# First MLP product ahead of the last two norms, a convolution's layer norm in two halves, and ties of a search counted from squared signs

## The chip, the cores and the metric

The kernel runs on one core of a Trainium2 chip. The metric is the device time of one execution in microseconds (us). The core has five engines that run side by side, each with its own instruction stream, held together by semaphores: PE (matrix products and transposes; PEld is its weight load), DVE, ACT and POOL (elementwise work), and SP (here only the issue of DMA transfers, in the order of its stream). Matrix products leave their results in eight PSUM banks; everything else lies in SBUF.

## The reference

One layer of a hybrid decoder on 1024 tokens of width 1024, all in float32. `h = rms_norm(x) @ w_in` is cut into inputs of three mixers, whose outputs, side by side, are multiplied by `w_out` and added to `x`; then cross-attention to 256 memory rows; then `x + relu(rms_norm(x) @ w1)**2 @ w2` with a hidden width of 4096.

```
y_a = gated_delta_rule(...)      # 4 heads of 128, chunks of 64, a state carried from chunk to chunk
y_b = sparse attention           # for every query the 256 keys with the largest index score:
      _, sel = lax.top_k(score, 256)              # of equal scores the lower positions win
y_c = silu(layer_norm(causal_depthwise_conv(u * sigmoid(gate), 31 taps) + bias) * g + b)   # 256 channels
x = x + concat(y_a, y_b, y_c) @ w_out
x = x + cross_attention(rms_norm(x), rms_norm(mem))
x = x + square(relu(rms_norm(x) @ w1)) @ w2
```

## The kernel before

**Arithmetic.** Matrix products are done at float32 precision from halves: each operand is split into a high part (a cast on ACT) and a low part (a subtraction on DVE), and `mm3` issues three matmuls for a pair: high by high (L133), first operand's high part by the second's low part (L134), and the first's low part by the second's high part (L135).

**Order.** Tokens are eight tiles `t` of 128 rows. The program is written as Python generators. `weave` interleaves several of them with a rate for each: the one with the higher rate emits more of its steps in the same stretch, and what is emitted first has the higher priority. A scheduler then sets the order on each engine from these priorities and from its own estimate of times; what runs on the chip is that fixed order per engine, and SP's DMA issues have one, too.

**The stretch from 383 to 547 us** is one such weave of four threads: the delta rule's preparation (`gdn_pre`, `gdn_blocks`, `gdn_post`; stages gp and gi, PSUM tag "mg"), the memory rows' norm and projection (`mem_norm`, `mem_stage`; tiles mem_mm, whi, mkv), the last steps of the search for the 256 keys (`topk`), and the convolution with its layer norm (`conv_norm`; the convolution is done with matmuls against diagonal matrices, tile diag). After it, from 547 to 765 us, the sparse attention (stage da) and the delta rule's scan (stage gs) are woven with the projection by `w_out`.

**The end of the search.** For every query block `b` of six, `lo` gets the sign of score minus threshold on ACT (L632), with the row's sum of signs; POOL writes `negm` = 1 where the sign is 0, a tie (L633); DVE makes running counts of ties `cs` (L635), works out how many ties still fit (L637, L638), marks what is left out (L640), and POOL turns it into the mask that is added later (L641). The tile `cs` has one buffer, so that the count of the next block waits for the L641 of the block before.

**The convolution's layer norm** (`conv_norm`): PE transposes the eight token tiles into four PSUM banks (L823), DVE takes mean and variance of each (L825, L826), then one `rsqrt` of ten small DVE instructions (L156 to L168) for all eight, eight scalings (L834), then for each half of four tiles the gain (L835), POOL's bias (L836), ACT's tanh (L838), the gate (L839) and a store `yc_d` (L840). The delta rule's block inverse is beside it on DVE: the chain of tiles `Tb`, `Pb`, `Wb` (L1001 to L1018), whose result is stored as `Xb_d` (L1020). `Ab_d` (L959) is the store, and `Ab` (L988) the load, which feed that chain. Behind the `Xb_d` store SP issues the loads of the attention (KA, VS) and of the scan (lvb, lkd, lqE, lqkT, lkT).

**The MLP** is done in four groups of 1024 hidden units, each as a seven-product scheme on 2 by 2 blocks (`PRODS`, order 1, 2, 5, 6, 3, 7, 4): a product is 48 matmuls of 128x512. `block_sums` makes sums of blocks of the weights (`wsum`) and of the normalised rows (`hsum`); `half` and `rows` split a block for a product (`wm` for weights, `bm` for rows; ACT casts at L1475, DVE subtracts at L1476). In the first group the weights' block sums run on POOL, and the rows' sums on DVE. Token tiles 6 and 7 ("rows 6 and 7") are the last to leave the cross-attention; their norm (n3) ends with transposes (L1412) and copies into the row blocks `h3` (L1415 on DVE, L1417 on ACT). Products 1 and 2 need only token tiles 0 to 3; product 5, the third, and the later ones need tiles 4 to 7 too. `mlp` is a generator that stops after its first product (`next(mlp)`), and rows 6 and 7 are normalised after that stop.

## Time and profile before

| | us |
|---|---|
| three runs | 1609.34, 1612.25, 1613.8 (median 1612.25) |
| the profiled execution | 1610.89 |
| its span, first to last instruction | 1609.2 |
| PE busy | 1513.7 (94%) |
| DVE busy | 1136.0 (71%) |
| ACT busy | 736.2 (46%) |
| POOL busy | 326.7 (20%) |
| mean granted clock of PE | 0.973 |

A row of the timeline gives start, duration, engine, line and operation, the tile written and read, shape, how many instructions are joined in the row, and in square brackets how long the engine was idle before it and what ended that wait. A row of the windows view gives for one stretch the busy time and number of instructions of each engine, PE's granted clock (1.00 is full speed), and the share and rate of DMA. A matmul's own duration overlaps with the next one's, so the pace of PE is read from the starts of its rows or from their number in a stretch in which it never stops.

### The profile page before, as it was taken

Reading aid. Unit: us, or ns where it says so; the run is one execution under the profiler, and the core shown is the slowest. Engines: PE = TensorE matmul, PEld = TensorE weight load, DVE = VectorE, ACT = ScalarE, POOL = GpSimd, SP = SyncE. Lnnn points to the kernel's source line nnn. Section 1 sums busy time; section 2 is a strip of 40 time slices with the busy share of each in tenths; the row PEclk is TensorE's granted clock in tenths of the full one; section 3 lists DMA queues with packets and bytes.
Section 4 is the critical chain, followed back from the end, with each engine's and each line's share of the span. In section 5 each row is a group of like instructions: output and inputs, shape, how many; then the busy total and the mean of one; then the engine's idle time right before and its main releaser. Section 6 shows DMA issues by size and latency. Waiting matters only on the chain.

```text
span 1609.2 us, 20703 instructions
## 1 busy us (share of the span) xinstructions
PE 1513.7 (94%) x7561; PEld 1261.1 (78%) x7561; DVE 1136.0 (71%) x2042; ACT 736.2 (46%) x1375; POOL 326.7 (20%) x279
## 2 busy tenths in 40 slices
PE   6999999998899599999879997999999999999998
PEld 6977888786689488988668876888888888888887
DVE  7649677875665766775667879996469647865783
ACT  4535788676443356664335533332233233323331
POOL 3021444346954222112301104100000000000000
PEclk9999999999899699999999998999999999999999
DMA  6130122121475864435612358713641464147202
GB/s 212 41 98 19 55 79 79 53 80 62 157 233 169 280 209 147 133 102 190 209 54 83 127 188 317 305 47 130 233 167 53 157 226 157 36 157 261 79 13 93
DMA packets 125141, 220.83 MB, mean 137 GB/s; under 512 B 16245, under 2 KB 65134, under 8 KB 117870
## 3 DMA queue, kind: packets, MB, share of 16 engines
q1 hardware_dynamic: 123502, 214.25, 38.9%
q0 software_dynamic: 1536, 5.24, 0.9%
q8 instruction: 60, 0.98, 0.2%
q14 instruction: 43, 0.35, 0.1%
HBM read 158.65 MB, written 60.82 MB: 136 GB/s over the span
## 4 chain that ended last, share of the span: by engine, by line
PE 65%; DVE 14%; ACT 9%; issue 5%; DMA 4%; POOL 3%; SPq 0%; ACTq 0%; POOLq 0%; DVEq 0%
PE mlp_mm L134 13%; PE mlp_mm L135 13%; PE mlp_mm L133 13%; ACT junka L592 4%; DVE acc L748 1%; PE xq_mm L133 1%; PE wa_mm L135 1%; PE wa_mm L133 1%; PE wa_mm L134 1%; PE xw_mm L135 1%; PE xw_mm L133 1%; PE xw_mm L134 1%; PE xq_mm L134 1%; PE xq_mm L135 1%; DVE junk L594 1%
## 5 line engine op out<-in xcount | busy, mean ns | idle before, releaser
L134 PE MATMUL mlp_mm<-bm,wm 128*128 128x512 f32 x448 | 178.5, 399 | 8.0 <-DVE bm L1476 8.0
L133 PE MATMUL mlp_mm<-bm,wm 128*128 128x512 f32 x448 | 177.7, 399 | 2.2 <-ACT bm L1475 1.2
L135 PE MATMUL mlp_mm<-bm,wm 128*128 128x512 f32 x448 | 178.2, 398 | 0.0
L135 PE MATMUL mlp_mm<-wm,am 128*128 128x512 f32 x448 | 177.0, 395 | 0.0
L134 PE MATMUL mlp_mm<-wm,am 128*128 128x512 f32 x448 | 177.0, 395 | 0.0
L133 PE MATMUL mlp_mm<-wm,am 128*128 128x512 f32 x448 | 175.0, 395 | 0.0
L1475 ACT CAST wm<-wq 128x2048 fp32r<-128x2048 f32 x32 | 61.2, 1912 | 211.9 <-PE mlp_mm L134 211.8
L1565 DVE TENSOR_TENSOR xacc<-xacc,mlp_mm 128x512 f32<-128x512 f32 x112 | 75.8, 682 | 69.7 <-PE mlp_mm L135 69.7
L134 PEld LDWEIGHTS mlp_mm<-bm,wm 128*128 128x128 f32 x448 | 85.0, 190 | 29.1 <-DVE bm L1476 8.7
L133 PEld LDWEIGHTS mlp_mm<-bm,wm 128*128 128x128 f32 x448 | 84.9, 190 | 23.3 <-DVE rs_x L156 1.5
L135 PEld LDWEIGHTS mlp_mm<-bm,wm 128*128 128x128 f32 x448 | 85.0, 190 | 20.3
L135 PEld LDWEIGHTS mlp_mm<-wm,am 128*128 128x128 f32 x448 | 84.1, 188 | 20.5
L134 PEld LDWEIGHTS mlp_mm<-wm,am 128*128 128x128 f32 x448 | 84.1, 188 | 20.4
L133 PEld LDWEIGHTS mlp_mm<-wm,am 128*128 128x128 f32 x448 | 84.1, 188 | 20.4
L1476 DVE TENSOR_TENSOR wm<-wsum,wm 128x2048 fp32r<-128x2048 f32 x24 | 59.3, 2472 | 51.3 <-ACT wm L1475 51.3
L1475 ACT CAST wm<-wsum 128x2048 fp32r<-128x2048 f32 x24 | 45.9, 1913 | 106.0 <-PE mlp_mm L134 77.7
L1476 DVE TENSOR_TENSOR wm<-wq,wm 128x2048 fp32r<-128x2048 f32 x32 | 73.3, 2290 | 28.6 <-ACT wm L1475 28.5
L133 PE MATMUL qkv_mm<-hT,whi 128*128 128x512 f32 x192 | 77.7, 404 | 0.9 <-ACT xb L740 0.9
L134 PE MATMUL qkv_mm<-hT,whi 128*128 128x512 f32 x192 | 76.7, 399 | 0.0
L135 PE MATMUL qkv_mm<-hT,wlo 128*128 128x512 f32 x192 | 76.7, 399 | 0.0
L1529 ACT ACTIVATE aq<-mlp_mm 128x512 f32<-128x512 f32 x64 | 37.9, 595 | 68.5 <-PE mlp_mm L135 68.5
L185 POOL TENSOR_TENSOR wlo<-wraw,whi 128x1024 fp32r<-128x1024 f32 x24 | 57.9, 2412 | 3.4 <-issue 1.9
(504 smaller groups left out, 3987.4 us busy)
## 6 DMA issues: line engine op xcount, KB each, us to landing
bm<-hb_d SPq DMA_DIRECT2D x42, 1024.0 KB, 6.5
wq<-in_mlp_w SPq DMA_DIRECT2D x32, 1024.0 KB, 5.3
hb_d<-bm SPq DMA_DIRECT2D x14, 1024.0 KB, 3.9
wraw<-in_w_in SPq DMA_DIRECT2D x20, 512.0 KB, 3.8
qkv_d<-acc SPq DMA_DIRECT2D x12, 512.0 KB, 3.2
...
xa<-in_x SPq DMA_DIRECT2D x16, 256.0 KB, 2.7
```

The source lines that it names most:

```text
L133: mm(out, l[0], r[0], start=start, stop=False, skip_group_check=on)
L134: mm(out, l[0], r[1], start=False, stop=False, skip_group_check=on)
L135: mm(out, l[1], r[0], start=False, stop=stop, skip_group_check=on)
L185: (lo_eng or nc.gpsimd).tensor_sub(lo[:, :n], raw[:, :n], hi[:, :n].bitcast(F32))
L592: Sc.activation(junka[:, :K], X[b], AF.Sign, bias=c, scale=-1.0, accum_out=n)
L594: V.tensor_scalar(junk[:, :K].bitcast(X[b].dtype), X[b], c, None, op0=OP.is_lt, op1=OP.add, accum_out=n)
L748: nc.vector.scalar_tensor_tensor(acc, xb[:, 3 - d:3 - d + T], self.cw[:, 3 - d, i:i + 1], acc, op0=OP.mult, op1=OP.add)
L1475: Sc.copy(w[0], x)
L1476: V.tensor_sub(w[1], x, w[0].bitcast(F32))
L1529: Sc.activation(x, ps[ch, m], AF.Relu if c == "21" else AF.Copy)
L1565: V.tensor_add(x, x, ps[ch, tt])
```

## The change

Three edits and new rates for the weave.

1. **Ties.** The tie marks are no longer written by POOL (L633) but by ACT as the square of the sign, which is 1 where there is no tie. DVE's running count subtracts a tile of ones (`onesb`, set once by POOL) so that it counts down at ties; the comparison and the constants change sign with it.
2. **Layer norm of the convolution** in two halves of four tiles: two PSUM banks for each half, a `rsqrt` for each half, a buffer of its own for the tanh. The rates of the weave go from 4.4, 2.6, 1.0, 6.0 to 4.0, 2.6, 1.3, 8.2 (delta rule, memory, search, convolution).
3. **Start of the MLP.** Product 1 of the first group is emitted ahead of the transposes of rows 6 and 7, and its evictions behind them. PSUM keeps four banks for the tag "mg" and four for "mm", and the stages `mlpg` and `mlp` share them out. The first two weight blocks go into a new pool `mlpw` instead of `blk`; the loads of the other two are issued behind the last store of `x3_d`. The weights' block sums of the first group run on DVE instead of POOL. The pools of the cross-attention are cut so that part of them is freed earlier.

```diff
-            nc.gpsimd.tensor_scalar(NEGM[b], sg, 0.0, 0.0, op0=OP.is_equal, op1=OP.add)
+            Sc.activation(NEGM[b], sg, AF.Square)
             cs = pool.tile([P, T], F32, name="cs", tag="kc", bufs=1)[:, :K]
-            V.tensor_tensor_scan(cs, NEGM[b], NEGM[b], 0.0, op0=OP.add, op1=OP.bypass)
-            V.tensor_add(r[:, j:j + 1], nsg[:, j:j + 1], cs[:, K - 1:K])
+            V.tensor_tensor_scan(cs, NEGM[b], onesb[:, :K], 0.0, op0=OP.add, op1=OP.subtract)
+            V.tensor_sub(r[:, j:j + 1], cs[:, K - 1:K], nsg[:, j:j + 1])
...
-        pts = []
-        mv = self.small.tile([P, NT, 2], F32, name="cmv")
-        for t in range(NT):
...
-        r = self.rsqrt(mv[:, :, 1], NT, 1.0, EPS, "rln")
         for n in range(2):
+            pts = [self.mm_ps([P, 2, 256]) for _ in range(2)]
+            mv = self.small.tile([P, 4, 2], F32, name="cmv")
+            for i in range(4):
...
+            r = self.rsqrt(mv[:, :, 1], 4, 1.0, EPS, "rln")
...
-            th = pool.tile([P, 4, 256], F32, name="cth", tag=f"cacc{n}")
+            th = pool.tile([P, 4, 256], F32, name="cth", bufs=1)
...
-            left = self.block_sums(V if g else G, q, {"new": new("wsum")}, False)
+            left = self.block_sums(V, q, {"new": new("wsum")}, False)
...
+                ahead = g == 0 and i == 0
...
+                    if not ahead:
+                        evict(ch, m, dst)
+                if ahead:
+                    yield 1.0
+                    for m in range(4):
+                        evict(ch, m, dst)
...
-        self.drain(self.weave((self.seq(*pre), 4.4), (self.seq(self.mem_norm(wu, mtp), self.mem_stage(wu, mkp)), 2.6),
-                              (topk, 1.0), (self.seq(conv, self.conv_norm(cva)), 6.0)))
+        self.drain(self.weave((self.seq(*pre), 4.0), (self.seq(self.mem_norm(wu, mtp), self.mem_stage(wu, mkp)), 2.6),
+                              (topk, 1.3), (self.seq(conv, self.conv_norm(cva)), 8.2)))
...
-                    if t - 2 < 6:
-                        self.norm_T(h3, t - 2, y3.pop(t - 2))
-            self.psum(0)
-            with sb_pool(tc, "mlp", bufs=1, side="right") as mp:
-                mlp = self.mlp(mp, (blk, blk2), h3, wq)
+                    self.norm_T(h3, t - 2, y3.pop(t - 2))
+                with tc.issue_after(self.x3_store.ins):
+                    w1_load(self.w1_blocks(0)[2:])
                 next(mlp)
                 for t in (6, 7):
                     self.norm_T(h3, t, y3.pop(t))
```

POOL's order at the end of the search, before. `negm_92` to `negm_97` are the masks of the six blocks, `zt` is the gate of the delta rule, `diag` a diagonal matrix of the convolution.

```order
L785 AFFINE_SELECT diag<-dwh 128x512
L785 AFFINE_SELECT diag<-dwl 128x512
L633 TENSOR_SCALAR negm_92<-lo_1197 128x384
L633 TENSOR_SCALAR negm_93<-lo_1198 128x512
L633 TENSOR_SCALAR negm_94<-lo_1199 128x640
L633 TENSOR_SCALAR negm_95<-lo_1200 128x768
L633 TENSOR_SCALAR negm_96<-lo_1201 128x896
L641 TENSOR_SCALAR negm_92<-cs 128x384
L633 TENSOR_SCALAR negm_97<-lo_1202 128x1024
L669 TENSOR_SCALAR zt<-zt,taps 128x512 x2
```

The same place now (line numbers are three higher, `junk` is the tile of ones).

```order
L629 MEMSET junk 128x1024
L672 TENSOR_SCALAR zt<-zt,taps 128x512
L788 AFFINE_SELECT diag<-dwh 128x512
L788 AFFINE_SELECT diag<-dwl 128x512
L644 TENSOR_SCALAR negm_92<-cs 128x384
L672 TENSOR_SCALAR zt<-zt,taps 128x512 x2
L644 TENSOR_SCALAR negm_93<-cs 128x512
L644 TENSOR_SCALAR negm_94<-cs 128x640
```

The six L633 are gone, one memset stands ahead, and the masks L644 (L641 before) follow each other more closely.

DVE's order at the end of the delta rule's block inverse, before, where its last links (Tb, Pb, Wb) stand among the statistics of the convolution's norm.

```order
L1013 TENSOR_TENSOR Tb<-Ab,Wb 128x512
L1050 COPY_PREDICATED Z_3452<-mask_3444,gi_mm 128x512
L1015 TENSOR_REDUCE Pb<-Tb 128x64
L825 BN_STATS cst<-cv_mm 128x6 x2
L1016 TENSOR_TENSOR Tb<-Wb,Pb 128x512
L826 BN_AGGR cmv<-cst 128x2 x2
L1018 TENSOR_REDUCE Wb<-Tb 128x8x8
L825 BN_STATS cst<-cv_mm 128x6 x2
L826 BN_AGGR cmv<-cst 128x2 x2
```

The same links now.

```order
L168 SCALAR_TENSOR_TENSOR rln_y<-rs_t,rs_y_4855 128x4
L1018 TENSOR_REDUCE Wb<-Tb 128x4x4
L833 TENSOR_SCALAR cyc<-cv_mm,cmv,rln_y 128x256 x4
L1013 TENSOR_TENSOR Tb<-Ab,Wb 128x512
L839 SCALAR_TENSOR_TENSOR cyc<-cth,cyc 128x1024
L835 TENSOR_TENSOR cyc<-cyc,conv_ln_g 128x1024
L145 TENSOR_TENSOR kvt_5057<-mkv_mm,kvt_5056 128x256
L1015 TENSOR_REDUCE Pb<-Tb 128x64
L1016 TENSOR_TENSOR Tb<-Wb,Pb 128x512
L1018 TENSOR_REDUCE Wb<-Tb 128x8x8
L839 SCALAR_TENSOR_TENSOR cyc<-cth,cyc 128x1024
```

The scalings, gains and gates of both halves, which stood behind the last L1018, now stand ahead of it, but for the last gate L839. On SP, behind the store of that result, stood before:

```order
L1020 DMA Xb_d_3468<-Wb_4933 128x256
L1669 DMA KA0_5116<-KA_d_152 128x1024
L1669 DMA KA1_5117<-KA_d_152 128x1024
L1670 DMA VS_5118<-VS_d_153 128x1024
L899 DMA lvb_5122<-gp_d_3469 128x512
```

And now:

```order
L1020 DMA Xb_d_3468<-Wb_5083 128x256
L1677 DMA KA0_5134<-KA_d_152 128x1024
L1677 DMA KA1_5135<-KA_d_152 128x1024
L840 DMA yc_d_86<-cyc_4868 128x4x256
L1678 DMA VS_5136<-VS_d_153 128x1024
L899 DMA lvb_5140<-gp_d_3469 128x512
```

The store of the convolution's second half, which needs the last L839, now stands ahead of VS and of every load of the scan.

DVE's order at the start of the MLP, before; `wm` are low parts of weights, `bm` low parts of rows, `n3y2` the norm of a token row. `bm_9762` belongs to product 1, `bm_9853` to product 2, `wm_9920` and `bm_9926` to the third.

```order
L1415 COPY h3_9535<-n3_mm_9830 128x4x128
L1437 TENSOR_TENSOR hsum_9923<-h3_9534,h3_9121 128x2048
L1476 TENSOR_TENSOR bm_9762<-h3_9121,bm_9761 128x2048
L1415 COPY h3_9535<-n3_mm_9842 128x4x128
L1449 TENSOR_TENSOR h3_9534<-h3_9535,h3_9534 128x2048
L1476 TENSOR_TENSOR wm_9920<-wsum_9752,wm_9919 128x2048
L1476 TENSOR_TENSOR bm_9853<-h3_9122,bm_9852 128x2048
L1476 TENSOR_TENSOR bm_9926<-hsum_9923,bm_9925 128x2048
L1443 TENSOR_TENSOR hsum_9923<-h3_9535,hsum_9923 128x2048
```

Now `bm_9778` (product 1), `bm_9873` (product 2), `wm_9941` and `bm_9947` (third) are the same tiles, and `wsum`, `wq` the weights' block sums.

```order
L1415 COPY h3_9567<-n3_mm_9762 128x4x128
L1476 TENSOR_TENSOR bm_9778<-h3_9142,bm_9777 128x2048
...
L196 SCALAR_TENSOR_TENSOR n3y2_9644<-x2_9706,n3_y_9753,g3_9016 128x1024
L1434 TENSOR_TENSOR wsum_9938<-wq_9768,wq_9770 128x2048
L1446 TENSOR_TENSOR wq_9768<-wq_9511,wq_9768 128x2048
L1476 TENSOR_TENSOR wm_9941<-wsum_9938,wm_9940 128x2048
L1476 TENSOR_TENSOR bm_9873<-h3_9143,bm_9872 128x2048
L1439 TENSOR_TENSOR wsum_9938<-wsum_9938,wq_9511 128x2048
L1415 COPY h3_9567<-n3_mm_9841 128x4x128
L1415 COPY h3_9567<-n3_mm_9853 128x4x128
L1437 TENSOR_TENSOR hsum_9944<-h3_9566,h3_9142 128x2048
```

The low part for product 1 has moved ahead of the two row norms (it stood behind them and behind a row sum), and three block sums of the weights have come into DVE's stream.

## Rows read from the trace of the kernel before

**Rows 1.** The page: PE's busy tenths in 40 slices of the span.

```profile
PE   6999999998899599999879997999999999999998
```

**Rows 2.** Windows: from:to, length, busy (count) per engine, PEclk, DMA share, GB/s.

```profile
385.00:415.00 30.00, 20.77 (x83) 15.76 (x82) 15.33 (x37) 14.49 (x27) 29.69 (x29) 0.84 0.18 54
530.00:547.00 17.00, 5.06 (x34) 3.58 (x32) 15.67 (x48) 2.16 (x6) 2.08 (x2) 0.75 0.88 299
547.00:567.00 20.00, 14.04 (x62) 12.32 (x63) 13.34 (x39) 11.51 (x27) 9.53 (x8) 0.53 0.95 338
958.00:1000.00 42.00, 30.76 (x121) 23.65 (x120) 40.85 (x32) 14.48 (x14) 17.71 (x3) 0.84 0.77 291
1000.00:1600.00 600.00, 600.00 (x2574) 483.09 (x2573) 433.23 (x348) 192.18 (x144) 7.21 (x1) 1.00 0.39 144
```

**Rows 3.** Timeline of PE at the MLP's start.

```profile
966.16 1.10 PE L1412 MATMUL n_mm<-ident,n3y 128*128 128x128 f32 x8 [0.96 <-DVE n3y L196]
972.03 0.80 PE L134 MATMUL mlp_mm<-bm,wm 128*128 128x512 f32 x1 [4.77 <-DVE bm L1476]
988.14 0.50 PE L134 MATMUL mlp_mm<-bm,wm 128*128 128x512 f32 x1 [3.23 <-DVE bm L1476]
```

**Rows 4.** Timeline of DVE at the MLP's start.

```profile
961.91 1.27 DVE L196 SCALAR_TENSOR_TENSOR n3y<-x,n_y,g 128x1024 f32<-128x1024 f32 x1
963.10 0.15 DVE L157 TENSOR_SCALAR rs_i<-rs_x 128x1 int32<-128x1 int32 x1
969.69 2.29 DVE L1476 TENSOR_TENSOR bm<-h,bm 128x2048 fp32r<-128x2048 f32 x1
972.61 6.64 DVE L1449 TENSOR_TENSOR h<-h,h 128x2048 f32<-128x2048 f32 x1
979.17 6.71 DVE L1476 TENSOR_TENSOR wm<-wsum,wm 128x2048 fp32r<-128x2048 f32 x1
```

**Rows 5.** Timeline of POOL and of SP's issues there.

```profile
972.50 4.60 POOL L1434 TENSOR_TENSOR wsum<-wq 128x2048 f32<-128x2048 f32 x1 [59.83 <-DMA wq<-in_mlp_w]
...
960.52 7.14 SPq L1499 DMA_DIRECT2D wq<-in_mlp_w  x5
```

**Rows 6.** Timeline of POOL and DVE at the end of the search.

```profile
384.01 11.65 POOL L633 TENSOR_SCALAR negm<-lo 128x384 bf16<-128x384 bf16 x5 [0.85 <-ACT lo L632]
397.33 4.61 POOL L633 TENSOR_SCALAR negm<-lo 128x1024 bf16<-128x1024 bf16 x1
...
397.28 1.23 DVE L635 TENSOR_TENSOR_SCAN cs<-negm 128x512 f32<-128x512 bf16 x1 [5.56 <-POOL negm L641]
```

**Rows 7.** Timeline of ACT there.

```profile
387.30 1.14 ACT L632 ACTIVATE lo<-SC,ih 128x1024 bf16<-128x1024 f32 x1
388.43 1.04 ACT L217 ACTIVATE whi<-wraw 128x1024 f32<-128x1024 f32 x1
402.22 1.15 ACT L219 ACTIVATE whi<-wraw,mem_y 128x1024 f32<-128x1024 f32 x1 [7.74 <-DVE mem_y L168]
```

**Rows 8.** Timeline of DVE, POOL, PE and SP at the end of the convolution's norm.

```profile
525.49 0.57 DVE L1001 TENSOR_TENSOR Tb<-Wb,Ab 128x4 f32<-128x4 f32 x1 [0.94 <-DMA Ab<-Ab_d]
542.98 3.71 DVE L834 TENSOR_SCALAR cyc<-cv_mm,cmv,rln_y 128x256 f32<-128x256 f32 x8
546.60 2.35 DVE L835 TENSOR_TENSOR cyc<-cyc,conv_ln_g 128x1024 f32<-128x1024 f32 x2
555.62 1.21 DVE L839 SCALAR_TENSOR_TENSOR cyc<-cth,cyc 128x1024 f32<-128x1024 f32 x1
...
547.96 5.51 POOL L836 TENSOR_TENSOR cyc<-cyc,conv_ln_b 128x1024 f32<-128x1024 f32 x2 [15.87 <-DVE cyc L835]
...
546.97 2.04 PE L1088 MATMUL gs_mm<-lvb,XT 128*128 128x128 f32 x8 [6.74 <-DVE cyc L834]
...
537.55 0.32 SPq L1020 DMA_DIRECT2D Xb_d<-Wb  x1
538.89 0.43 SPq L1670 DMA_DIRECT2D VS<-VS_d  x1
```

More of the change, by code (lines that the diff above doesn't have):

```diff
@@ L116, in mm_ps @@
     def mm_ps(self, shape, name="mm"):
-        own = self.gbanks and self.stage in ("gp", "gi", "gs", "gn", "xq", "xp")
+        own = self.gbanks and self.stage in ("gp", "gi", "gs", "gn", "xq", "xp", "mlpg")
         t = self.ps.tile([P, 512], F32, name=f"{self.stage}_{name}", tag="mg" if own else "mm",
@@ L626, in topk @@
         for j, b in enumerate(order):
-            V.memset(half[:, j:j + 1], 256.0 - (b + 1) * 64)
+            V.memset(half[:, j:j + 1], (b + 1) * 64 - 256.0)
+        onesb = junk.bitcast(BF)
+        nc.gpsimd.memset(onesb, 1.0)
         for j, b in enumerate(order):
@@ L1329, in cross_qT @@
             self.nc.tensor.transpose(pt[:, h], qc[:, h], self.ident)
-        qT = [self.xl.tile([P, H, P], F32R, name=f"xqT{i}", bufs=2) for i in range(2)]
+        qT = [self.xt.tile([P, H, P], F32R, name=f"xqT{i}", bufs=2) for i in range(2)]
         self.split(qT[0], qT[1], pt)
@@ L1366, in cross_o @@
             h = hp * 2 + i
-            PT = [self.xl.tile([P, 2, 256], F32R, name=f"xPT{j}", bufs=2) for j in range(2)]
+            PT = [self.xq.tile([P, 2, 256], F32R, name=f"xPT{j}", bufs=2) for j in range(2)]
             pt = self.mm_ps([P, 2, 256])
@@ L1553, in mlp @@
                 l, r, ch, dst = self.PRODS[p]
+                self.stage = stages[ch == 0]
                 l, r = act(left(l)), half(right(r))
@@ L1709, in h3_blocks @@
                     h3[f"{g + 1}{n + 1}"] = blk.tile([P, 4, 512], F32, name="h3", tag="blk")
-            with sb_pool(tc, "xl", bufs=1, side="right") as xl, sb_pool(tc, "xe", bufs=1, side="right") as xe, \
-                    sb_pool(tc, "wr", bufs=1, side="right") as wr, \
-                    sb_pool(tc, "xq", bufs=1, side="right") as xp:
-                self.xl = xl
+            with ExitStack() as xs:
+                xas = xs.enter_context(ExitStack())
+                xl = xas.enter_context(sb_pool(tc, "xl", bufs=1, side="right"))
+                xbs = xas.enter_context(ExitStack())
+                self.xt, xe, wr, xq = (xbs.enter_context(sb_pool(tc, x, bufs=1, side="right")) for x in ("xt", "xe", "wr", "xq"))
+                xp = xl
+                self.xl, self.xq = xl, xq
                 def raw():
@@ L1753, in run @@
                     if i < NT:
-                        yT[i] = self.out_rows(xp, i, *rows.pop(i))
+                        yT[i] = self.out_rows(xq, i, *rows.pop(i))
                         if i + 2 < NT:
@@ L1786, in run, with w1_load @@
                         Pm[i - 4] = self.cross_p(xp, qT.pop(i - 4), kT)
+                xbs.close()
+                wpool = bs.enter_context(sb_pool(tc, "mlpw", bufs=1))
+                w1 = []
+                def w1_load(srcs):
+                    for src in srcs:
+                        w1.append(wpool.tile([P, 4, 512], F32, name="wq", bufs=5))
+                        nc.sync.dma_start(w1[-1], src)
+                w1_load(self.w1_blocks(0)[:2])
+                pools = []
+                mlp = self.mlp(wpool, pools, (blk, blk2), h3, w1)
                 for t in range(NT + 6 - W0, NT):
@@ L1801, in run @@
                     self.norm_T(h3, t, y3.pop(t))
+                xas.close()
+                pools.append(xs.enter_context(sb_pool(tc, "mlp", bufs=1, side="right")))
                 self.drain(mlp)
```

73 lines of the change are left out of this document (33 added, 40 removed).

## The prediction

> **What bounds the kernel now.** I read the page's slices first [rows 1]: PE, busy for 94% of the span, is at 9 tenths nearly everywhere, and below that in a few places: the tenth and eleventh slice (362 to 442 us), the fourteenth (523 to 563), two from 764 to 845, one at 965, and the ends. So PE bounds the kernel, and only an edit that fills one of PE's holes, or opens one, moves the end. Next the windows of the holes that the change touches [rows 2]: idle time of PE is length less busy time, 9.2 us in 385 to 415 at a mean clock of 0.84, 11.9 in 530 to 547 at 0.75, 6.0 in 547 to 567 at 0.53, 11.2 in 958 to 1000 at 0.84. Where the clock reads about 0.5 it is at 1.2 GHz, and a matmul takes twice as long: 547 to 567 loses about 14.0 × 0.47 = 6.6 us by that too. From 1000 us PE never stops (600.00 of 600): 2574 matmuls, 0.233 us each, so that 48 of a product take 11.2 us. Last I read, in the timelines, what each hole waits for [rows 3 to 8].
>
> **Start of the MLP, before.** PE does four matmuls of product 1, then waits until 972.03, and after four of product 2 until 988.14, for low parts `bm` from DVE [rows 3]. Product 2's other 44 matmuls take 10.3 us, and some 1.5 more at the lower clock (an estimate from the window's 0.84): the third product starts at about 1000, where the full window begins. DVE is the reason: 40.85 of 42 us busy [rows 2]. Two of its operations take 6.64 and 6.71 us where the like takes 2.29 alone [rows 4]; they run beside POOL's block sums [rows 5]. The first starts at 972.61 inside POOL's sum of 972.50 to 977.10 and ends 2.2 us after it: it waited for POOL to end, then ran its 2.29.
>
> The Trainium skill (SBUF — State Buffer, "Who interferes with whom") states this as an exclusive lock: a DVE operation with two SBUF inputs and a POOL operation that reads SBUF block one another for the whole instruction. The row agrees: 977.10 + 2.29 = 979.39 against 979.25 measured. By plain sharing of bandwidth a sum moved to DVE would cost it about what it saves, and only the 7.8 us of the earlier low part's place would count for product 1, so that the time would be near the 1609 of the second rival; by the lock DVE is rid of waits of some 4.4 us each, and the sum below stands.
>
> **Start of the MLP, after.** DVE's order gives its times. The low part for product 1 follows the copy L1415, so from 961.9 [rows 4] to 964.2, against 969.69 + 2.29 = 972.0. Behind it come two L196 of 1.27 and ten small operations at a pace of about 0.2: to about 968.7. Then two block sums, `wm_9941` and `bm_9873`, four of 2.29, to about 978; the third sum to 980; the copy that frees the PSUM bank of product 2's second matmul, to 981. Then the row sum, evictions and the next low part `bm_9947` (two of 2.29, two of about 0.68 and 1.28, L1449) to about 991, and the one for the fourth product to 1002.
> PE: 44 matmuls from 964.2 end at 974.5, sixteen transposes (8 take 1.10, [rows 3]) at 976.7. Product 2 is held by the bank until 981 and ends near 991.7; the third, whose low part came at 991, ends near 1003; the fourth, ready at 1002, ends near 1014. Before, the fourth ended at 1000 + 22.4 = 1022.4. The gain is 8 us. DVE is then no longer late, since after 1000 us it is busy 433 of 600.
> What can take from it: the two weight blocks that DVE now sums at 968.7. Before, five loads were issued from 960.52 on and POOL had the first two at 972.50 [rows 5]; now they are issued a little earlier (ahead of a store of `bm`) with fewer others behind them. If they land 8 us after issue, at about 968.5, nothing is lost; at 972.5 all of DVE's stream, product 2's copy included, is 4 us late. Bounds: 3 (late loads, and DVE's handovers costing a us more) to 11 (the hole of 11.2 gone). I take 8.
>
> **Ties.** POOL loses six L633, 11.65 + 4.61 = 16.3 us [rows 6], in a stretch where it is busy 29.69 of 30 [rows 2]. ACT gets six squares, priced as the six L632 beside them (1.14 for the widest [rows 7]): at most 6.8 us, on an engine half idle there (14.49 of 30). The memset has no row there; below it stands nothing, above it a POOL pass over 1024 columns, 4.61; I take 1 of it, beside free time of POOL. DVE's count reads two bf16 tiles as before: no change, up to one more L635 (1.2 us) if a second source should cost. What goes is the wait of 5.56 us of the second count on POOL's L641; behind that on DVE stands the norm of the memory rows, for which ACT waits 7.74 [rows 7] and then PE. So the 9.2 us hole shrinks. The rest (masks L641, still one buffer for `cs`) stays. I take 6 us earlier at PE, between 0 and 11 (hole plus clock).
>
> The Trainium skill (ScalarE: Activation LUTs, "Table sets: the hidden batching unit") speaks against sign and square by turns: a switch to another set costs about 2.7 us, and twelve would put 32 us on ACT. But L217, a square, starts at 388.43, where L632, a sign, ends (387.30 + 1.14), with no table load between them [rows 7]. By the row the price is zero; by the page, if the sets differed, the 6 us would be gone.
>
> **Layer norm in halves.** Ten more small operations, 2 us of DVE. What it moves weighs more. Before, the scan's first matmul waited until 546.97 for the scalings that freed PSUM (start 542.98), and two gains and two gates followed until 556.8 [rows 8], while PE stood and its clock was at 0.53 to 0.75. Now that work is done ahead. But it stands in DVE's order between the links of the block inverse that the scan needs: from the first link to the store `Xb_d` it took 537.55 − 525.49 = 12.1 us [rows 8]; now some 5 us of norm come into it (a gain 1.18, a gate 1.21, four scalings 1.9, a second `rsqrt` 2, less statistics that have gone ahead), and about 4 ahead of it. With PE some 4 us earlier there (6, less 2 for work moved ahead), I put that store at about 543. Behind it the second half's yc store now stands ahead of VS and the scan's loads: the last gate is one POOL pass (2.8 [rows 8]), a tanh and 1.21 behind a gain, 2 to 3 us later than the last link. Before, the scan's first matmul came 9.4 us behind the store (546.97 − 537.55); with the same, the loads later and the wait for PSUM gone, it comes at about 552, 5 us later. Against that stand the DVE work of 546.6 to 556.8, gone from behind it, and PE work (projection of the memory rows, first steps of scan and preparation) that lies ahead of it and fills the 11.9 us hole. Half of what 547 to 567 loses, 6 of 12.6, covers the delay. For ties and norm together I take 0, between −9 (scan late, nothing back) and +11.
>
> **The sum.** 1610.89 for the profiled execution less 8 is 1603; that execution lies 1.4 us under the median of the runs shown, so 1612.25 − 8 = 1604.
>
> **Rivals.**
> *Both holes before 567 close.* The weave puts the memory projection into the 11.9 us hole and the clock stays up. For it: PE's wait was for PSUM held by the scalings, and this reason is gone. Against: Xb_d and the loads behind it, and DMA, busy 0.88 to 0.95 of that time. 11 more: 1593.
> *The MLP gains little.* Weight blocks land at 972.5 as before, DVE paces the first four products: 3 us, 1609. For it: the rows of POOL's start; against: fewer loads in the queue.
> *Slower: the store in front of the loads.* On SP the yc store of the second half stands ahead of VS and of the scan's loads. It decides alone: before, that gate ended at 556.83 and VS was issued at 538.89 [rows 8]. If the gate comes no earlier, VS is issued 18 us later, and what PE won in the ties is only waited out: 1612.25 − 8 + 18 = 1622. It is slower by more than 5 us when VS goes later than 538.89 + 8 + 5 = 552. Against: the gate's order on DVE right behind the last link.
> *The ties don't come off*: ACT needs table loads, the masks stay as late; then the scan is 5 us later: 1609.
>
> **How the numbers follow.** My forecast 0.50, both holes 0.15, little in the MLP 0.15, ties not 0.07, the store 0.13. A measurement of this kernel can tell 0.3%, 5 us, from no change. The forecast's own range is 1598 to 1610: nine tenths of it is faster (0.45), so is the first rival (0.15) and a sixth of the two small gains (0.03): 0.63. Within: 0.05 + 0.19 + 0.02 = 0.26. Slower: 0.11, from the store. The range goes down to the first rival, 1594, and up past the small gains to 1614; it leaves out about 0.07 below and 0.11 above.
>
> **What would show it.** Right: PE's transposes of rows 6 and 7 behind 48 matmuls, L1476 alone at 2.29 throughout, the fourth product over at about 1014 less what came before; no POOL row over 5 us in the search; no table load beside the squares; PE over 24 of 30 busy in 385 to 415. Wrong: block sums of DVE waiting on `wq`; VS issued later than 546; scan's first matmul later than 555 with PE idle ahead of it.

## The result, and the profile after

| | before | after |
|---|---|---|
| median us (4 runs each) | 1611.26 | 1594.24 (1590.78 to 1596.08) |
| profiled execution | 1610.89 | 1596.08 |
| its span | 1609.2 | 1594.3 |
| PE / DVE busy | 1513.7 / 1136.0 | 1500.4 / 1113.8 |
| ACT / POOL busy | 736.2 / 326.7 | 739.3 / 286.0 |

The ratio is 0.9891, interval 0.9877 to 0.9905: about 17 us faster, where 8 had been forecast. Two executions of the kernels below, of 2024.91 us (before_128_up) and 2499.85 us (gz_off_sp_no_norm, whose trace is of it and isn't read here), ran at a mean granted clock of 0.69 and 0.56 and count in no median. The first surprise is PE's busy time. No edit takes matmuls away, both runs have the mean clock 0.973, and yet PE is busy 13.3 us less.

PE's slices after; they answer to [rows 1].

```profile
PE   6999999997999489999889998999999999999999
```

Of the two slices below nine tenths from 362 to 442 us one is left (359 to 399, 7 tenths instead of 8), the hole at 523 is now at 518 and deeper (4 tenths instead of 5), and the one at 965 is smaller (8 instead of 7). The windows after, which answer to [rows 2]:

```profile
385.00:415.00 30.00, 21.77 (x91) 17.35 (x90) 17.75 (x43) 17.34 (x33) 17.70 (x21) 0.83 0.30 98
530.00:547.00 17.00, 4.16 (x37) 3.93 (x35) 15.50 (x38) 3.75 (x6) 5.92 (x4) 0.74 0.45 151
547.00:567.00 20.00, 9.83 (x68) 9.04 (x69) 3.02 (x12) 3.73 (x13) 0.00 (x0) 0.71 1.01 367
958.00:1000.00 42.00, 36.73 (x158) 29.10 (x157) 39.82 (x39) 17.78 (x18) 0.00 (x0) 0.92 0.71 266
1000.00:1600.00 600.00, 590.36 (x2553) 479.37 (x2552) 425.76 (x346) 187.86 (x141) 0.00 (x0) 1.00 0.40 147
```

POOL lost its 12 us in 385 to 415 and PE won only 1.0 there. From 530 to 567 PE is idle 12.84 + 10.17 = 23.0 us, against 17.9. From 958 to 1000 it is busy 36.73 instead of 30.76, at 0.92 instead of 0.84. The last window now holds the end of the kernel.

**MLP start.** PE and DVE, which answer to [rows 3, 4]:

```profile
959.44 1.19 PE L133 MATMUL mlpg_mm<-bm,wm 128*128 128x512 f32 x4 [0.82 <-ACT bm L1475]
963.79 0.80 PE L134 MATMUL mlpg_mm<-bm,wm 128*128 128x512 f32 x1 [3.16 <-DVE rs_x L156]
...
976.02 1.91 PE L1412 MATMUL n_mm<-ident,n3y 128*128 128x128 f32 x16
...
978.84 0.50 PE L134 MATMUL mlp_mm<-bm,wm 128*128 128x512 f32 x1 [0.16 <-DVE bm L1476]
...
991.24 0.51 PE L134 MATMUL mlp_mm<-bm,wm 128*128 128x512 f32 x1 [1.13 <-DVE bm L1476]
```

```profile
961.45 2.28 DVE L1476 TENSOR_TENSOR bm<-h,bm 128x2048 fp32r<-128x2048 f32 x1
...
969.76 2.29 DVE L1434 TENSOR_TENSOR wsum<-wq 128x2048 f32<-128x2048 f32 x1 [1.83 <-DMA wq<-in_mlp_w]
972.09 2.29 DVE L1446 TENSOR_TENSOR wq<-wq 128x2048 f32<-128x2048 f32 x1
...
980.90 1.28 DVE L1415 COPY h<-n_mm 128x512 f32<-128x512 f32 x2
...
988.90 2.28 DVE L1476 TENSOR_TENSOR bm<-hsum,bm 128x2048 fp32r<-128x2048 f32 x1
...
1000.11 2.28 DVE L1476 TENSOR_TENSOR bm<-hsum,bm 128x2048 fp32r<-128x2048 f32 x1
```

The low part of product 1 is made at 961.45, and PE's 4.77 and 3.23 us of waiting are now 3.16, 0.16 and 1.13. DVE's operations of 2048 columns take 2.28 or 2.29 throughout. Its first block sum waits 1.83 us for a weight block, no more.

**Front.** PE, SP and DVE at the end of the convolution's norm, which answer to [rows 8]:

```profile
555.52 2.05 PE L1088 MATMUL gs_mm<-lvb,XT 128*128 128x128 f32 x8 [21.36 <-DMA lvb<-gp_d]
```

```profile
544.69 0.32 SPq L1020 DMA_DIRECT2D Xb_d<-Wb  x1
...
546.47 0.37 SPq L840 DMA_DIRECT2D yc_d<-cyc  x1
546.90 0.49 SPq L1678 DMA_DIRECT2D VS<-VS_d  x1
547.44 0.89 SPq L899 DMA_DIRECT2D lvb<-gp_d  x1
```

The load `lvb` in before, which [rows 8] don't have:

```profile
539.36 0.43 SPq L899 DMA_DIRECT2D lvb<-gp_d  x1
```

```profile
535.49 1.89 DVE L833 TENSOR_SCALAR cyc<-cv_mm,cmv,rln_y 128x256 f32<-128x256 f32 x4
...
538.23 1.22 DVE L839 SCALAR_TENSOR_TENSOR cyc<-cth,cyc 128x1024 f32<-128x1024 f32 x1
539.36 1.22 DVE L835 TENSOR_TENSOR cyc<-cyc,conv_ln_g 128x1024 f32<-128x1024 f32 x1
...
543.98 0.69 DVE L1018 TENSOR_REDUCE Wb<-Tb 128x64 f32<-128x512 f32 x1
544.58 1.22 DVE L839 SCALAR_TENSOR_TENSOR cyc<-cth,cyc 128x1024 f32<-128x1024 f32 x1
```

DVE's last link L1018 comes at 543.98, with four scalings, a gate and a gain between the links, and SP's store `Xb_d` at 544.69. The second half's store and VS stand in front of the scan's loads; `lvb` goes out at 547.44 and takes 8 us with DMA full (share 1.01). So the scan starts at 555.52, where it had started at 546.97. Of the 8.1 us by which `lvb` is later, 7.1 are the later `Xb_d`; from `Xb_d` to `lvb` it is 2.75 us instead of 1.81.

**Search.** ACT and PE, which answer to [rows 6, 7]:

```profile
390.04 3.23 ACT L635 ACTIVATE negm<-lo 128x384 bf16<-128x384 bf16 x5
393.18 1.04 ACT L217 ACTIVATE whi<-wraw 128x1024 f32<-128x1024 f32 x1
...
399.12 1.15 ACT L219 ACTIVATE whi<-wraw,mem_y 128x1024 f32<-128x1024 f32 x1 [2.90 <-DVE mem_y L168]
```

```profile
400.32 0.47 PE L229 MATMUL mem_mm<-ident,whi 128*128 128x128 f32 x1 [8.23 <-ACT whi L219]
```

Five squares take 3.23 us together, straight behind the signs and with a square L217 straight behind them. But L217 begins the norm of the memory rows, and it starts at 393.18 now, where it started at 388.43 [rows 7]. L219, behind DVE's small operations of that norm, follows at 399.12, and PE waits 8.23 us in one piece for it.

### The profile page after: what moved, and what is told of

The parts are those of the page before. It is cut to its first block, busy times and chain, and to the rows that moved or that the text cites. A ratio compares the mean times of both kernels' runs of the same rounds, so it can differ in the third digit from the quotient of the medians.

```text
span 1594.3 us, 20703 instructions
## 1 busy us (share of the span) xinstructions
PE 1500.4 (94%) x7561; PEld 1257.0 (79%) x7561; DVE 1113.8 (70%) x2056; ACT 739.3 (46%) x1381; POOL 286.0 (18%) x270
## 4 chain that ended last, share of the span: by engine, by line
PE 66%; DVE 10%; ACT 10%; issue 6%; DMA 4%; POOL 4%; SPq 0%; POOLq 0%; ACTq 0%; DVEq 0%
PE mlp_mm L134 6%; PE mlp_mm L135 6%; PE mlpg_mm L135 6%; PE mlpg_mm L134 6%; PE mlp_mm L133 6%; PE mlpg_mm L133 6%; ACT junka L592 4%; DVE acc L751 1%; PE gi_mm L1049 1%; PE xq_mm L133 1%; PE xw_mm L135 1%; PE xw_mm L133 1%; PE xw_mm L134 1%; PE xq_mm L134 1%; PE xq_mm L135 1%
## 5 line engine op out<-in xcount | busy, mean ns | idle before, releaser
L134 PE MATMUL mlpg_mm<-bm,wm 128*128 128x512 f32 x256 | 101.4, 396 | 3.2 <-DVE rs_x L156 3.2
L135 PE MATMUL mlpg_mm<-bm,wm 128*128 128x512 f32 x256 | 101.6, 397 | 0.0
L134 PE MATMUL mlp_mm<-wm,am 128*128 128x512 f32 x256 | 101.2, 396 | 0.0
L135 PE MATMUL mlp_mm<-wm,am 128*128 128x512 f32 x256 | 101.2, 395 | 0.0
L133 PE MATMUL mlpg_mm<-bm,wm 128*128 128x512 f32 x256 | 99.3, 392 | 0.8 <-ACT bm L1475 0.8
L133 PE MATMUL mlp_mm<-wm,am 128*128 128x512 f32 x256 | 99.3, 396 | 0.0
L1476 DVE TENSOR_TENSOR wm<-wsum,wm 128x2048 fp32r<-128x2048 f32 x24 | 54.9, 2287 | 50.1 <-ACT wm L1475 50.1
L1573 DVE TENSOR_TENSOR xacc<-xacc,mlp_mm 128x512 f32<-128x512 f32 x64 | 43.4, 683 | 49.1 <-PE mlp_mm L135 49.1
L134 PE MATMUL mlp_mm<-bm,wm 128*128 128x512 f32 x192 | 75.4, 393 | 1.3 <-DVE bm L1476 1.3
L133 PE MATMUL mlpg_mm<-wm,am 128*128 128x512 f32 x192 | 75.9, 396 | 0.0
L134 PE MATMUL mlpg_mm<-wm,am 128*128 128x512 f32 x192 | 75.9, 396 | 0.0
L135 PE MATMUL mlpg_mm<-wm,am 128*128 128x512 f32 x192 | 75.9, 396 | 0.0
L135 PE MATMUL mlp_mm<-bm,wm 128*128 128x512 f32 x192 | 75.1, 394 | 0.0
L133 PE MATMUL mlp_mm<-bm,wm 128*128 128x512 f32 x192 | 74.7, 390 | 0.0
L134 PEld LDWEIGHTS mlpg_mm<-bm,wm 128*128 128x128 f32 x256 | 48.6, 190 | 14.9 <-DVE rs_x L156 3.6
```

Source lines behind the costliest of these rows:

```text
L133: mm(out, l[0], r[0], start=start, stop=False, skip_group_check=on)
L134: mm(out, l[0], r[1], start=False, stop=False, skip_group_check=on)
L135: mm(out, l[1], r[0], start=False, stop=stop, skip_group_check=on)
L1476: V.tensor_sub(w[1], x, w[0].bitcast(F32))
L1573: V.tensor_add(x, x, ps[ch, tt])
```

## Experiments

Each ratio is against runs of the kernel before beside it on the same chip.

### Which part does it

`mlp_only` is the kernel before with the third edit alone, `front_only` the one with the first two and the new rates.

> The kernel before with the third edit alone (start of the MLP, pools, PSUM tags, weights' block sums on DVE). Left-hand tiles in SBUF keep their places, modulo 256 bytes at 0x60. Theory A: the start of the MLP is worth 9 us, and the quicker pace of the matmuls of the up products (0.229 us instead of 0.233) comes from where the tiles lie in SBUF, which this kernel doesn't move: 1611.3 - 9 = 1602, up products at 0.233. Theory B: the pace comes with the third edit (four PSUM banks for each of two tags, evictions later, POOL free): 1611.3 - 9 - 6 = 1596, up products at 0.229.

> The kernel before with the first two edits (ties, layer norm in halves) and the rates of the weave, without the third. Its tile of mean and variance is 64 bytes smaller over both buffers, so that every tile on the left of SBUF lies 64 bytes lower, at 0x20 modulo 256. Theory A: up products at 0.229 although nothing in the MLP is changed: 1344 matmuls x 0.0043 = 6 us, and 0 to 3 us from the stretch of 385 to 570 us and from other products with the same pace: 1605, between 1602 and 1606. Theory B: pace 0.233, 1611 within 2.

Measured: 1615.54, ratio 1.0028 [1.0017, 1.0039], and 1610.41, 0.9989 [0.9976, 1.0001]. Both theories on mlp_only missed, and front_only came out near the second. Neither part alone is faster, and together they are by 17 us. In mlp_only the MLP's start does gain (7.5 us in the trace), but some 10 are lost in the cross-attention (below). The other thing that belongs to no part was the pace of PE behind 1000 us.

### The pace of the 128x512 matmuls

The MLP has two kinds of stretches of 78 us: products with `w1` (up: `bm` moves, `wm` is stationary) and with `w2` (down: `wm` moves, `am` is stationary). Windows inside an up, then a down stretch, at full clock and with PE busy throughout, of before:

```profile
1137.00:1207.00 70.00, 70.00 (x302) 56.32 (x301) 43.66 (x37) 22.37 (x21) 0.00 (x0) 1.00 0.55 203
1060.00:1130.00 70.00, 70.00 (x302) 56.31 (x301) 53.94 (x44) 19.91 (x11) 0.00 (x0) 1.00 0.30 106
```

of after:

```profile
1127.00:1197.00 70.00, 70.00 (x307) 57.47 (x306) 44.91 (x39) 23.11 (x22) 0.00 (x0) 1.00 0.54 203
1050.00:1120.00 70.00, 70.00 (x301) 56.40 (x300) 54.09 (x44) 20.11 (x11) 0.00 (x0) 1.00 0.29 106
```

Up products now fit 307 where there were 302; down products are the same. From start to start of neighbouring rows (those under 0.25 us apart) an up matmul of the second to fourth group takes 0.2289 us instead of 0.2333. On 1344 of them that is 5.9 us; the projections before the MLP show smaller gains of the same kind (`qkv` 0.2325 to 0.2291, `xq` 0.2325 to 0.2297). Nothing in the edits touches these matmuls. What changed is where their operands lie: the second edit's `cmv` has half the size and two buffers, 64 bytes less in a pool that lies below nearly all others on the left side of SBUF. All left-hand tiles (`bm`, `am`) moved from 0x60 to 0x20 modulo 256, and the right-hand ones (`wm`) stayed at 0xe0. One product has both operands on the left and so at equal places, the first of the first group, whose `wm` lies in `blk`. In before its last steps are quicker than those of all others, 24 steps of 0.227 us between these two starts:

```profile
977.90 0.39 PE L135 MATMUL mlp_mm<-bm,wm 128*128 128x512 f32 x1
...
983.35 0.39 PE L134 MATMUL mlp_mm<-bm,wm 128*128 128x512 f32 x1
```

To test this I added unused bytes to the pool of constants, which moves the left side and leaves the order of every engine as it is:

```diff
-        self.one = self.consts.tile([P, 1], F32, name="one")
+        self.one = self.consts.tile([P, 1], F32, name="one"); self.consts.tile([P, 16], F32, name="pad")
```

(16 words are 64 bytes; 128 and 192 bytes likewise; in after_right_192 the bytes lie on the right side, in after_both_c0 on both; before_128_up is the kernel before.)

> The changed kernel with 64 unused bytes in the pool of constants, so that every left-hand tile lies at 0x60 modulo 256 as in the kernel before; every engine's order is the same. Theory A: the up products, the qkv and the query products go back to 0.233: 1594.2 + 5.8 + up to 3 = 1600 to 1603. Theory B: no change, 1594 within 2.

> The changed kernel with 192 unused bytes in the pool of constants: left-hand tiles at 0xe0 modulo 256, the same as the right-hand ones; orders the same. Theory A in its form A1, the pace depends on how the places of the two operands differ modulo 256 (equal is quick): both up and down products at 0.229, 1594.2 - 5.8 = 1588. Form A2, it depends on the moving operand's own place (0x20 quick, 0x60 and 0xe0 slow): up products back at 0.233, 1600 to 1603. Theory B: 1594 within 2.

> The kernel before with 128 unused bytes: left-hand tiles at 0xe0 modulo 256 as the right-hand ones, orders the same. If the pace is a matter of places alone, both kinds of MLP product come down from 0.233 to 0.2267 as in the changed kernel with 192 bytes: 2592 x 0.0065 = 17 us, and 4 to 6 more from qkv, query and output products: 1611.3 - 17 - 5 = 1589. If the third edit's PSUM tags take part, less than half of it: 1600 or more.

> The changed kernel with 128 unused bytes: left-hand tiles at 0xa0 modulo 256, right-hand ones at 0xe0; orders the same. If the pace goes by the difference of moving less stationary place modulo 256 (0x00: 0.227, 0x40: 0.229, 0x80 and 0xc0: 0.233, as the runs so far have it), the up products (0xc0) go at 0.233 and the down products (0x40) at 0.229: 1594 within 3. If it goes by the moving operand's place alone, the down products stay at 0.233.

> The changed kernel with 192 unused bytes on the right of SBUF: both sides at 0x20 modulo 256, the left-hand tiles where the changed kernel has them; orders the same. By the difference, which is now zero: both kinds of product at 0.227, 1580 within 3. By the place of the left-hand tiles alone: no change, 1594.

> The changed kernel with 160 unused bytes on the left and 32 on the right: all tiles at 0xc0 modulo 256, thus at multiples of 64 bytes, which none had so far; orders the same. If only equality counts: 0.227 and 1580 within 3. If a start on a multiple of 64 counts too: quicker than 0.227, below 1577.

| kernel | left, right mod 256 | up us | down us | median us | ratio |
|---|---|---|---|---|---|
| before | 60, e0 | 0.2330 | 0.2333 | 1611.26 | 1 |
| after_64_up | 60, e0 | 0.2330 | 0.233 | 1603.87 | 0.9949 [0.9936, 0.9963] |
| after | 20, e0 | 0.2289 | 0.2333 | 1594.24 | 0.9891 [0.9877, 0.9905] |
| after_128_up | a0, e0 | 0.2332 | 0.2289 | 1593.66 | 0.9884 [0.9865, 0.9903] |
| before_128_up | e0, e0 | 0.2267 | 0.2267 | 1591.15 | 0.987 [0.9856, 0.9885] |
| after_right_192 | 20, 20 | 0.2268 | 0.2267 | 1582.61 | 0.9826 [0.9802, 0.9849] |
| after_both_c0 | c0, c0 | 0.2268 | 0.2267 | 1583.11 | 0.9824 [0.981, 0.9839] |
| after_192_up | e0, e0 | 0.2268 | 0.2267 | 1580.34 | 0.9808 [0.9794, 0.9822] |

With the old places the change comes out where the forecast said: 1603.87. The other 9.6 us come and go with 64 unused bytes. With both operands at one place modulo 256, before itself gains 20 us, and the changed kernel 23.5 over its run with the old places (1603.87 to 1580.34). The same windows in after_192_up, up and down:

```profile
1120.00:1190.00 70.00, 70.00 (x311) 57.96 (x310) 45.59 (x40) 23.10 (x22) 0.00 (x0) 1.00 0.55 199
1043.00:1113.00 70.00, 70.00 (x310) 57.96 (x310) 54.99 (x45) 20.75 (x11) 0.00 (x0) 1.00 0.30 106
```

and in after_128_up, where up is slow again and down has become quick:

```profile
1127.00:1197.00 70.00, 70.00 (x301) 56.40 (x300) 43.66 (x37) 21.60 (x21) 0.00 (x0) 1.00 0.55 207
1050.00:1120.00 70.00, 70.00 (x308) 57.43 (x307) 55.70 (x45) 21.11 (x12) 0.00 (x0) 1.00 0.29 103
```

In these runs the pace goes by moving less stationary address modulo 256: 0x00 gives 0.2267 us, 0x40 0.2289, 0x80 and 0xc0 0.233. Whether both lie at a multiple of 64 (c0, c0) doesn't matter, only that they are equal. front_only is an exception, with places as in after and an up pace that changes from group to group; the same pairs of buffers and banks come up in its quick and its slow groups. Windows in its second and third up stretch:

```profile
1138.00:1208.00 70.00, 70.00 (x302) 56.71 (x301) 43.64 (x37) 22.13 (x21) 0.00 (x0) 1.00 0.55 204
1295.00:1365.00 70.00, 70.00 (x307) 57.46 (x306) 44.93 (x39) 23.13 (x22) 0.00 (x0) 1.00 0.55 203
```

I suspected the division of PSUM, which the third edit changes, and gave front_only that division:

```diff
-        own = self.gbanks and self.stage in ("gp", "gi", "gs", "gn", "xq", "xp")
+        own = self.gbanks and self.stage in ("gp", "gi", "gs", "gn", "xq", "xp", "mlpg")
...
```

(with the tags set by product as in the third edit).

> The first two edits alone as in front_only, tiles at 0x20 and 0xe0, and in the MLP the PSUM tags mg and mm of four banks each by product as in the third edit, instead of eight banks in rotation; product 1 and DVE's work stay as before. In front_only the up products of groups 1 and 3 went at 0.229, those of 2 and 4 at 0.233. If the division of PSUM takes part in the pace, all four groups go at 0.229: 672 x 0.0043 = 3 us less than front_only's 1610.4, 1607. If not, two of four at 0.233 and 1610 within 2.

Measured: 1609.46, 0.9993 [0.9976, 1.001], with the same pattern from group to group. The division of PSUM has no part in it. So the difference of places is not the whole rule, and what slows every second up stretch of front_only stays open.

### The start of the MLP

```diff
-            left = self.block_sums(V, q, {"new": new("wsum")}, False)
+            left = self.block_sums(V if g else G, q, {"new": new("wsum")}, False)
```

> The changed kernel with the weights' block sums of the first MLP group on POOL again, as before. By the lock that the prediction read from the rows, DVE waits for whole POOL instructions again (operations of 6.6 us instead of 2.29), the low parts of the second to fourth product come later: 3 to 6 us lost at the start of the MLP, 1594.2 + 4.5 = 1599. Rival: DVE has the time, since it is rid of four sums of 2.29; nothing is lost, 1594 within 2.

Measured: 1605.23, 0.9956 [0.9944, 0.9968], 11 us behind after and more than either theory gave; 7.5 of them are lost from the MLP's start on in the trace. Moving the sums to DVE is thus most of the third edit's worth, although DVE is the engine that was short there. DVE and POOL of this run:

```profile
978.33 4.83 DVE L1476 TENSOR_TENSOR wm<-wsum,wm 128x2048 fp32r<-128x2048 f32 x1 [8.90 <-ACT wm L1475]
...
986.49 5.43 DVE L1437 TENSOR_TENSOR hsum<-h,h 128x2048 f32<-128x2048 f32 x1
```

```profile
976.44 4.58 POOL L1446 TENSOR_TENSOR wq<-wq 128x2048 f32<-128x2048 f32 x1
983.25 6.53 POOL L1439 TENSOR_TENSOR wsum<-wsum,wq 128x2048 f32<-128x2048 f32 x1 [2.23 <-DVE wm L1476]
```

Two of DVE's operations are stretched again, and both end 2.1 us behind POOL's (983.16 and 981.02, 991.92 and 989.78), where alone they take 2.28. That fits the lock that the prediction cites (the Trainium skill, SBUF — State Buffer, "Who interferes with whom"), as do 6.64 us beside POOL's sums [rows 4] and 2.28 without. But the stretching is 5.7 us in sum, and DVE also waits 8.90 us for a cast of POOL's first sum: POOL takes 4.6 us for a sum that takes DVE 2.29. How much of the 7.5 us is the lock and how much POOL's pace, this run does not separate.

### The front

`ties_only` is before with the first edit; `norm_only_64_up` has the second edit with its rates, and `halves_old_rates_64_up` the halves with the rates of before, both with 64 unused bytes so that the places are those of before.

> The kernel before with the first edit alone (ties from squared signs on ACT); tiles keep their places. My prediction gave the ties up to 6 us at PE in the stretch of 385 to 415. Theory C (the ties gain, the norm in halves and the rates lose): 1611.3 - 4 = 1607, PE busy over 24 of the 30 us of 385 to 415. Theory D (POOL's relief is taken up by another wait, the gain is nought): 1611 within 2. In both the up products stay at 0.233.

> The kernel before with the second edit and the rates of the weave alone, and 64 unused bytes that bring the tiles back to the places of the kernel before (0x60 modulo 256). The changed kernel with 64 bytes more spent 5.6 us more than the kernel before between the last qkv product and the last w_out product of the first part. Theory C: this is the norm's and the rates' loss, with the ties' gain taken off: 1611.3 + 6 to 10 = 1617 to 1621, and the scan's first matmul 5 to 12 us later than the 547 of before. Theory D: 1611.3 + 3 to 6.

> The norm in two halves alone, with the old rates of the weave, and 64 unused bytes that keep the tiles at the places of the kernel before. norm_only_64_up, with the new rates, had 1619.1 against 1611.8. Theory G (the halves put norm work between the links of the block inverse whatever the rates): 1617 to 1620, the scan's first matmul at 555 or later. Theory H (the rates 8.2 and 4.0 do it, which bring the convolution ahead of the preparation): 1611 within 3, the scan at 545 to 549.

Measured: 1607.07, 0.9974 [0.9963, 0.9985]; 1619.11, 1.0038 [1.0026, 1.005]; 1613.16, 1.001 [0.9996, 1.0024]. The ties give 4 us, the scan starting at 543.1. The norm with its rates costs 6 (scan at 559.9). The halves alone cost nothing clear, though the scan starts at 553.3, 6 us later than in before and later than theory H had it. So most of the cost is the rates', and about half of the scan's delay.

To see whether the stores on SP hold the scan's loads, the `yc_d` stores and the second `Xb_d` store went to POOL's queue, at equal places:

```diff
-            nc.sync.dma_start(self.yc_d[n * 4:n * 4 + 4].rearrange("t p c -> p t c"), yc)
+            nc.gpsimd.dma_start(self.yc_d[n * 4:n * 4 + 4].rearrange("t p c -> p t c"), yc)
...
-        nc.sync.dma_start(self.Xb_d[n:n + 4].rearrange("n b j i -> (n b) (j i)"), W[:, 0:256])
+        (nc.gpsimd if n else nc.sync).dma_start(self.Xb_d[n:n + 4].rearrange("n b j i -> (n b) (j i)"), W[:, 0:256])
```

> The changed kernel with 192 unused bytes (1580), and the second Xb_d store and the yc_d stores issued by POOL instead of SP, so that on SP the loads of KA, VS and the scan stand behind no store that waits for DVE. In the changed kernel PE stands from 534.2 to 555.5 for the load lvb, issued at 547.4 behind these stores. Theory E (the queue's order makes the hole): lvb is issued near 540 or earlier, the scan starts at 545 to 549, 6 to 9 us won: 1573. Theory F (DMA, full at that time, or DVE's links set the start): the loads come earlier and land no earlier, or the scan then waits for XT: 1580 within 3.

Measured: 1578.57, 0.9797 [0.9775, 0.9818], not clear of after_192_up. `lvb` goes out at 543.75 and still takes 7.5 us to land, the scan starts at 551.2. The run doesn't free the loads, though: ahead of them on SP stand stores of the memory rows, for which it waits 3.6 us on DVE's L145, and the load `yci` (L1242), which waits 1.8 us for the moved `yc_d` store itself. What speaks for a small part of the store in front are the rows of after above, 0.9 us of 8.1; the rest is the later `Xb_d`, behind links between which DVE now does the norm.

### The 10 us of the cross-attention

no_norm_192_up has edits 1 and 3 with the norm and rates of before, at equal places.

> The ties and the start of the MLP without the norm in halves and with the old rates, and 128 unused bytes that put left-hand and right-hand tiles at 0xe0. Sum of the parts measured alone: 1611.5 - 4.4 (ties) - 9.5 (MLP start) - 20.5 (places) = 1577, if the 10 us that the third edit alone lost in the cross-attention's first rows (wait for xr, 765 to 785 us) do not come back; 1587 if they do. The changed kernel with the same places had 1580.

Measured: 1589.53, 0.9864 [0.9847, 0.988], near the 1587 given for the case that the 10 us are lost here too. PE waits 15.2 us for `xr` (L1299), as in mlp_only, whose PE and SP show:

```profile
780.98 1.11 PE L1277 MATMUL wb_mm<-ident,yai 128*128 128x128 f32 x4 [14.83 <-DVE xr L1296]
```

```profile
770.98 0.34 SPq L1267 DMA_DIRECT2D gz<-gz_d  x1
...
771.96 1.11 SPq L1290 DMA_DIRECT2D xr<-x_d  x2
```

The load of `xr` stands in SP's order behind a `gz` load, for which SP waited 15.6 us on POOL's `yT`. I moved two rows' `gz` and `ya` loads to POOL, in that kernel and in after_192_up with the old rates:

```diff
-        q = self.nc.gpsimd if t < 2 else self.nc.sync
+        q = self.nc.gpsimd if t < 4 else self.nc.sync
```

> The kernel of no_norm_192_up (edits 1 and 3, norm and rates as before, equal places; 1589.5 us) with one change: the loads gz and ya of token tiles 2 and 3 (L1267 and its neighbour) are issued by POOL's queue instead of SP's. Theory (SP's queue: the gz load waited there for POOL's yT, and the g and xr loads stood behind it): PE's idle time of some 15 us at the first cross-attention product goes down to under 6 and the time is 1579 to 1581. Rival (xr itself is late, because what it reads is written late or because DMA is full): the idle time stays over 12 and the time is 1588 to 1590.

> Edits 1, 2 (the halves, with the weave's rates of the kernel before) and 3, equal places, and the loads gz and ya of token tiles 2 and 3 on POOL's queue. If the new rates cost 6 us as in halves_old_rates_64_up against norm_only_64_up, and no stall of xr is left: 1580.3 - 6 = 1574. If the cost of the rates is only that of the front and is given back in the cross-attention: 1580.

Measured: 1586.83, 0.9848 [0.9834, 0.9861], and 1583.26, 0.9826 [0.9813, 0.984]. The numbers of all theories on the two were missed. The second kernel's SP and PE show why:

```profile
758.16 0.34 SPq L1267 DMA_DIRECT2D gz<-gz_d  x1
...
761.95 0.81 SPq L1290 DMA_DIRECT2D xr<-x_d  x2
```

```profile
769.86 1.11 PE L1277 MATMUL wb_mm<-ident,yai 128*128 128x128 f32 x4 [12.98 <-DVE xr L1296]
```

The next row's `gz` load has taken the place of the one that I moved. Behind it `xr` waited 2.3 us more, for the scan's last store `ya_d` of `oc`: since the third edit recut the pools, the first buffer of `xr` (163808) is the memory of `oc`'s second; before it lay at 118752. The last kernel moves all those loads to POOL and swaps `xr` with the rows `n2_y`, which come later:

```diff
-        q = self.nc.gpsimd if t < 4 else self.nc.sync
+        q = self.nc.gpsimd
...
                 g2 = xp.tile([P, D], F32, name="g2")
+                xl.tile([P, D], F32, name="n2_y", tag="n2_y", bufs=2)
```

> Edits 1, 2 (the halves, with the weave's rates of the kernel before) and 3, equal places, all loads gz and ya on POOL's queue, and the two buffers of xr laid where the rows n2_y lay, away from the memory of the scan's last output oc. In gz_off_sp_old_rates SP's gz load still waited for POOL's yT until 758.16, and xr behind it until 761.95 for the store ya_d of oc, whose memory xr takes since edit 3; PE lost 13 us (1583.26). Theory (both waits together are the cause): xr is issued before 755, PE's idle time there goes under 6 and the time is 1574 to 1577. Rival (xr comes earlier, but PE then waits for the weights wslot, whose loads and splits fill DMA and POOL from 743 to 766): 1580 to 1583.

Measured: 1578.28, 0.9796 [0.978, 0.9812].

```profile
749.32 0.91 SPq L1290 DMA_DIRECT2D xr<-x_d  x2
```

```profile
763.24 1.11 PE L1277 MATMUL wb_mm<-ident,yai 128*128 128x128 f32 x4 [6.74 <-DVE xr L1296]
```

```profile
758.97 3.61 DVE L1229 TENSOR_TENSOR wslot<-wraw,wslot 128x1024 fp32r<-128x1024 f32 x1 [2.02 <-ACT wslot L1228]
762.50 2.47 DVE L1296 TENSOR_TENSOR xr<-xr,wb_mm 128x512 f32<-128x512 f32 x4
```

`xr` is issued 12.6 us earlier, and PE's wait falls from 12.98 to 6.74. The time lies between what the two theories gave, and so does the cause: the two waits were half of it. The rest is a part of the rival's, the weights' splits: DVE's L1296 now stands straight behind a split of `wslot` (L1229), which waits 2.02 us for ACT and then takes 3.61 us, beside a split of POOL's, where another took 1.22 us 3 us earlier.

This stretch is also a large part of why the parts don't add up. From 740 to 790 PE is busy 41.28 us in before, 32.15 in mlp_only and 43.75 in after: the third edit's loss doesn't show beside the other two. Why the new rates end the scan earlier (744.5 in after_192_up against 751.6 in xr_own_place) though it starts later, I did not test; it makes up for what they cost in front, since the old rates did not make the whole faster (1583.26 against 1580.34).

## Why the prediction missed the size

**The sum without pace was met, in part by luck.** With the tiles at their old places the change takes 1603.87 us; 1604 was forecast. But in that trace the MLP's start gains 9.1 us, and 3.8 are lost ahead of it, where 8 and 0 had been taken (its first matmul starts at 963.98 against 960.17, the fourth product is over at 1017.0 against 1022.3). And the 10 us that the third edit alone loses in the cross-attention were in no term; that they don't show beside the other two edits was not foreseen. The first rival's 1593 is close to the 1594.24 measured by chance: it wanted both holes before 567 us closed, and there PE was idle longer.

**The step that failed** is the sentence "From 1000 us PE never stops (600.00 of 600): 2574 matmuls, 0.233 us each", taken as the same after. It has no term in the sum. It should have had one: the change makes and cuts pools, so tiles move, and 64 bytes were worth 9.6 us, more than the whole forecast. The row itself gave no hint; the hint stood in other products of the same shape: in the profile before, the end of the MLP's first product goes at 0.227, and of the steps of `wa` 90 of 157 take under 0.228, where the MLP's other products go at 0.233.

**MLP start: right.** 8 us, with the fourth product over at 1014. Its first matmul starts at 1001.9 and 48 take 11: over at 1012.9, against 1022.4. Of these 9.5 us, 0.7 had been won ahead of the MLP and some 0.8 are pace (192 matmuls); 8 are left. Of the steps, the third product's low part came at 991.2 (991 in the working), the fourth's at 1002.4 (1002). One was wrong and did no harm: product 2 was not held for its bank until 981 but ran from 977.69 with one wait of 0.16, and the third product waited for its low part instead. DVE's sums waited 1.8 us for weight blocks, one of the three signs named as wrong, and it cost nothing.

**Ties: right in kind, under the forecast.** No table load, no POOL row over 5 us; 4 us instead of 6. "PE over 24 of 30 busy in 385 to 415" was wrong: 21.77, and 21.95 in ties_only. POOL's stream was not what PE waited for there. The six squares were put "on an engine half idle there", at no cost to PE; but five of them stand ahead of L217, which starts at 391.94 in ties_only against 388.43, and PE waits 8.04 us there for the L219 behind it.

**Norm in halves: right in its path, short in size.** `Xb_d` went out at 544.69 (543 forecast), the scan started at 555.52 (552). The other two signs named as wrong came true as well, VS later than 546 (546.90) and the scan later than 555. The 6 us that were to come back there did not do so as idle time: PE's grew by 5.1 us, though its clock was higher (0.71 against 0.53 in 547 to 567). By the single runs the rates did most of the cost, and I had given them no price. Ties and norm together cost 2 by these runs (6 less 4) where I took 0. Of the slower rival little appeared: VS went out 8.0 us later, but 7.1 of that is the later `Xb_d`, and the store in front added under 1 of its 18.
